# A list scheduler with new durations, a shared-port clock, more homes for filler weights, and a bias sum moved from ScalarE to VectorE

## The chip, the cores and the metric

The kernel runs on one core of a Trainium2 chip. The core has a matrix engine (TensorE, PE in the profile, with its weight loads as PEld), VectorE (DVE), ScalarE (ACT), GpSimd (POOL) and SyncE (SP), from whose queue every DMA of this kernel is issued. They share one memory of 128 partitions (SBUF); PE writes its results to eight accumulation banks (PSUM). The metric is the device time of one execution in microseconds.

## The reference, cut to what matters

One layer of a hybrid backbone over 1024 tokens of width 1024, with 256 context tokens. A modulated RMS norm is followed by one input projection; from it come a Fourier branch and a gated DeltaNet in two directions; both are merged by gates, and a ConvFFN of width 2816 follows. The part that the change touches is the DeltaNet's decay matrix:

```python
gc = jnp.cumsum(chunks(g), axis=-1)
decay = jnp.exp(jnp.where(lower_incl, gc[..., :, None] - gc[..., None, :], -jnp.inf))
kk = jnp.einsum('nbhcd,nbhsd->nbhcs', kc, kc)
l_mat = jnp.where(lower_strict, bc[..., :, None] * kk * decay, 0.0)
sol = lax.linalg.triangular_solve(l_mat, rhs, left_side=True, lower=True, unit_diagonal=True)
```

The kernel forms the decay as exp(-|g_j - g_i|) on a full 128 by 128 block and uses the triangle that it needs.

## The kernel before, in words

**A program that is recorded, ordered and then emitted.** `layer` calls engine methods, but these only record an `Op` (L172) with its operands and a `cost` (L247). `gates` adds what buffers impose: a tile in a region waits for the last reader of the tile that lay there before. `schedule` (L351) then walks a clock of its own: each engine has a time at which it is free, an operation is ready when its predecessors end plus a latency, and among those ready the one with the longest chain behind it (`rank`) goes next. The outcome is a fixed order on each engine, and the chip runs each engine's instructions strictly in that order, with waits between engines. So a number in `cost` moves no instruction's duration on the chip; it moves places in the order. All instructions carry the line of the one emitting call, L349 (L360 in the changed file), which is why the profile's groups are told apart by engine, tile kind and shape.

**The stages of the first half.** Ten stages in `ORDER` (two of context, c0 and c1, eight heads, x0 to x7) each go through: `project_kv` or `kq_head` (projections of 128 by 512 pieces, each value split in a high and a low part, hence three matmuls for a product), `decay_products`, `invert_blocks` (31 short VectorE steps), `merge_blocks` (chains of 32x32 and 64x64 matmuls named pa, pb, pc, pdd, pee) and a scan (`step`, L995: matmuls X and Y with VectorE and ScalarE between them). These chains leave PE without work, so a later stage's projections and the *fillers* of `side` (L1137: products z, g1, g0 and f that only the second half needs) are put between them.

**Fillers.** The weights of one filler are two halves of 128 by 512. Each half is loaded, copied rounded on ScalarE (the high part, tag `fh`) and subtracted on VectorE (the low part, in place of the load, tag `fl`). `WB` (L30) gives the number of homes: two for `fh`, three for `fl`. Results of all fillers go through one PSUM bank; the second group of 512 columns starts when ScalarE has evacuated the first.

**The decay (L796).** For each of two directions, a tile F of 128 by 8 by 128 is loaded with the row of cumulated logs broadcast over the partitions. Eight ScalarE instructions take |F + bias|, one for each 128 columns because the bias is another column vector each time; one more takes exp(-F). VectorE then multiplies F into the products kk, which start the inversion.

**The second half.** From about 1000 us on: output projections, then the FFN by a scheme of seven products with sums of weights on GpSimd (`both`, L1585), a 3 by 3 convolution on VectorE (`conv`, L1635), and the down projection.

Of the kernel before, what the change touches and what calls it, by code (L numbers as in the profile page):

```python
# [10 lines left out]
F32R = mybir.dt.float32r  # L11
AF = mybir.ActivationFunctionType
ALU = mybir.AluOpType
# [3 lines left out]
P = 128  # L17
# [9 lines left out]
AHEAD = 50  # L27
HALF = 512
WORDS = 53200
WB = {"H": 8, "L": 8, "h": 3, "l": 3, "fh": 2, "fl": 3, "woh": 8, "wol": 8, "dh": 3, "dl": 3, "LT": 2, "tk": 2}  # L30
DB = {"kn": 1, "vn": 1, "fs": 1}
ORDER = ("c0", "x0", "x1", "c1", "x2", "x3", "x4", "x5", "x6", "x7")
SIDES = (4, 4, 2, 2, 2, 2, 2, 2, 2, 2)
# [136 lines left out]


class Op:  # L172
    __slots__ = ("eng", "method", "args", "kw", "cost", "preds", "succs", "n", "ready", "rank", "start", "at", "ins", "bonus")

    def __init__(self, eng=None, method=None, args=(), kw=None, n=-1, cost=0.0):
        self.eng, self.method, self.args, self.kw, self.n, self.cost = eng, method, args, kw, n, cost
        self.preds, self.succs, self.ready, self.start, self.bonus = {}, [], 0.0, None, 0.0


def _meet(a, b):  # L180
# [8 lines left out]
class Program:  # L189
# [57 lines left out]
    def cost(self, eng, method, args, kw):  # L247
        out = args[0] if args else kw["out"]
        shape = out.shape
        n = math.prod(shape[1:])  # L250
        ins = [x for x in list(args[1:]) + list(kw.values()) if isinstance(x, View)]
        psum = any(v.slot.space == PSUM for v in ins)
        if eng == "PE":
            if method == "transpose":
                return max(53, args[1].shape[0] * 2 / 2.4 + 2)
            rhs, m = args[2], math.prod(args[1].shape[1:])
            n = max(math.prod(rhs.shape[1:]), m)
            if rhs.shape[0] <= 64 and m <= 64:
                return 34 if n <= 32 else 80
            return n / 2.4 + 3 if rhs.dtype == F32R and n >= 256 else n * 4 / 2.4 + 5  # L260
        if eng == "DVE":
            if method == "reciprocal":
                return 65 + 6.3 * n
            ptr = any(v.shape[-1] == 1 and v.arr.size <= P for v in ins) and method in ("tensor_scalar", "scalar_tensor_tensor")
            fast = method in ("tensor_copy", "tensor_scalar") and not psum and out.slot.space != PSUM
            return 66 + n / (1.92 if fast else 0.96) + (61 if ptr else 0)
        if eng == "ACT":
            aps = any(isinstance(kw.get(x), View) for x in ("scale", "bias", "accum_out"))
            return (51 if psum else 93) + n * 0.833 + (93 if aps else 0)
        if eng == "POOL":  # L270
            if method == "memset":
                return 36 + 0.83 * n
            if kw.get("op") == ALU.pow:
                return 300 + 165 * n
            if method == "tensor_copy":
                return 119 + 3.33 * n
            if method == "affine_select":
                return 1060
            return 140 + 2.12 * n
        run = 1  # L280
        view = out if isinstance(out, View) else args[1]
        if isinstance(view, View):
            a_ = view.arr
            for d in range(a_.ndim - 1, -1, -1):
                if a_.shape[d] > 1 and a_.strides[d] != run:
                    break
                run *= a_.shape[d]
        total = math.prod(shape) * 4
        return max(60.0, total / 359.0 * (1 if run * 4 >= 512 else 2))

    def record(self, engine, method, args, kw):
        op = Op(engine.name, method, args, kw, len(self.ops), self.cost(engine.name, method, args, kw))
        op.bonus = self.bonus
        out = args[0] if args else kw["out"]
        for k_, v in list(enumerate(args[1:])) + list(kw.items()):
            if isinstance(v, View) and k_ not in ("out", "accum_out"):
                self.access(op, v, False)
        for v in (out, kw.get("accum_out")):
            if isinstance(v, View):
                self.access(op, v, True)  # L300
        self.ops.append(op)
# [49 lines left out]
    def schedule(self):  # L351
# [7 lines left out]
        while todo:  # L359
            o = todo.pop()  # L360
# [11 lines left out]
            done += o.cost if o.eng == "PE" else 0.0  # L372
        left = {o: len(o.preds) for o in nodes}
        free = {n: 0.0 for n in self.eng}
        cold = 0.0
        wait, can = {n: [] for n in self.eng}, {n: [] for n in self.eng}
        count, dma, hw = 0, 0.0, 0.0
        issued = []
# [19 lines left out]
        for _ in range(len(ops)):  # L398
            best = None
            for n in self.eng:  # L400
                if can[n]:
                    t = free[n]
                elif wait[n]:
                    t = max(free[n], wait[n][0][0])
                else:
                    continue
                if best is None or t < best[0]:
                    best = (t, n)
            t, n = best
            while wait[n] and wait[n][0][0] <= t + AHEAD:  # L410
                _, c, o = heapq.heappop(wait[n])
                heapq.heappush(can[n], (-o.rank, c, o))
            o = heapq.heappop(can[n])[2]
            t = max(t, o.ready)
            o.start = t
            issued.append(o)
            if n == "SP":
                hw = max(hw, t + 50) + 460
                dma = max(dma, hw + 700) + o.cost
                free[n] = max(t + 60, dma - LEAD)  # L420
                end = dma
            else:
                cost = o.cost
                if n == "PE":
                    if t - free[n] > 3000:
                        cold = t + 4500
                    if t < cold:
                        cost *= 2
                free[n] = end = t + cost
            work = []  # L430
            for q in o.succs:
                settle(q, end + self.lat(o, q), work)
            release(work)
# [54 lines left out]
def layer(prog, a, out):  # L488
    te, ve, se, po, sp = (prog.eng[n] for n in ("PE", "DVE", "ACT", "POOL", "SP"))
# [4 lines left out]
    psum = pool("psum", bufs=2, space=PSUM)  # L494
# [143 lines left out]
    for q in range(4):  # L638
        n = (2, 4)[q // 2]
# [149 lines left out]
    NU = 8  # L789
# [6 lines left out]
    def decay_products(name, kT, co, cols, growsrc, qT=None):  # L796
        rk, b2, bk, c1 = co
        gcol = cols(ngc)
        Fs, LTs = [], []
        for d in range(2):  # L800
            F_ = dt("F", f"F_{name}{d}", (P, NU, P))
            src = growsrc(d)
            Ff = F_.rearrange("p u j -> p (u j)")
            sp.dma_start(Ff.rearrange("p (a b) -> p a b", a=src.shape[1]) if len(src.shape) == 3 else Ff, src)
            for u in range(NU):
                se.activation(F_[:, u, :], F_[:, u, :], AF.Abs, bias=gcol[:, d, u:u + 1])
            se.activation(F_, F_, AF.Exp, scale=-1.0)
            Fs.append(F_)
            LTs.append(dt("LT", f"L_{name}{d}", (P, NU, P)))
        for g in range(2):  # L810
            pt = ps("pd", [P, 4, P], f"kk_{name}{g}")
            for i in range(4):
                u = g * 4 + i
# [984 lines left out]
```

## Time and profile before

| | |
|---|---|
| median of three runs | 2051.59 us (2049.98 to 2053.32) |
| the profiled execution | 2047.95 us, its span 2046.2 us |
| PE busy | 1953.0 us, 95% |
| VectorE, ScalarE, GpSimd busy | 67%, 42%, 28% |
| mean granted PE clock | 0.979 |

PE is busy almost throughout. What is to be read is therefore where PE is not busy, what ended each such wait, and where its clock was granted at half. The profile's `m`, `p` and `d` stand for SBUF, PSUM and DRAM tiles; idle time in brackets is that just ahead of an instruction, with what ended it.

### The profile page before, as it was taken

What the parts mean: (1) busy time and instruction counts of PE and PEld (TensorE: products, weight loads), DVE (VectorE), ACT (ScalarE), POOL (GpSimd) and SP (SyncE); (2) the same over time, 40 slices, a digit from 0 to 9 for tenths busy, and PEclk for the clock granted to TensorE, in tenths of its full rate; (3) what the DMA queues carried; (4) which work ended last, traced back from release to release, by engine and by line L of the source; (5) the groups of instructions that cost most, each with busy time, mean ns of one, the idle gap of its engine ahead of it and who ended that gap; (6) DMA issues with size and microseconds to landing.
All of it is one profiled execution on the core that took longest, in us unless ns stands there. A gap on an engine that the chain in (4) does not pass through costs nothing.

```text
span 2046.2 us, 31495 instructions
## 1 busy us (share of the span) xinstructions
PE 1953.0 (95%) x11470; PEld 1570.9 (77%) x11470; DVE 1363.1 (67%) x2848; ACT 858.1 (42%) x2088; POOL 564.0 (28%) x573
## 2 busy tenths in 40 slices
PE   8989999899999999999999999979999999999998
PEld 3868888787777788778776778857878888878886
DVE  5648767667677577673655485479988889882132
ACT  5575354555354453632431032454444444532121
POOL 3110121101112220210221000257878888600000
PEclk9989999899999999999999999999999999999999
DMA  7153324344451543441778562312222222453231
GB/s 298 52 187 92 105 88 132 117 145 128 113 149 52 149 150 92 118 114 51 223 234 289 181 221 102 114 52 78 95 75 80 83 83 86 167 181 100 77 126 52
DMA packets 180637, 257.52 MB, mean 126 GB/s; under 512 B 75921, under 2 KB 97522, under 8 KB 180482
## 3 DMA queue, kind: packets, MB, share of 16 engines
q1 hardware_dynamic: 180482, 255.51, 39.0%
q8 instruction: 90, 1.47, 0.3%
q14 instruction: 65, 0.53, 0.1%
HBM read 194.52 MB, written 60.94 MB: 125 GB/s over the span
## 4 chain that ended last, share of the span: by engine, by line
PE 71%; DVE 14%; DMA 5%; ACT 5%; issue 2%; POOL 1%; SPq 0%; DVEq 0%; POOLq 0%; ACTq 0%
PE p L349 71%; DVE m L349 11%; ACT m L349 4%; DMA m<-d 3%; DVE p L349 3%; DMA d<-m 2%; ACT p L349 1%; POOL m L349 1%; DMA m<-in_w_ada_dram 1%; SPq L349 0%; DMA m<-in_wu_dram 0%; ACT L349 0%; DVEq L1787 0%; POOLq L1787 0%; DVEq L349 0%
## 5 line engine op out<-in xcount | busy, mean ns | idle before, releaser
L349 PE MATMUL p<-m,m 128*128 128x512 f32 (+7 forms) x11310 | 1937.8, 338 | 75.7 <-ACT m L349 31.6
L349 PEld LDWEIGHTS p<-m,m 128*128 128x128 f32 (+4 forms) x11310 | 1551.2, 174 | 452.6 <-ACT m L349 62.4
L349 DVE TENSOR_TENSOR m<-m,m 128x512 fp32r<-128x512 f32 (+27 forms) x1096 | 557.4, 523 | 253.4 <-ACT m L349 222.8
L349 ACT ACTIVATE m<-m 128x512 fp32r<-128x512 f32 (+8 forms) x649 | 411.3, 652 | 613.5 <-DMA m<-d 161.0
L349 POOL TENSOR_TENSOR m<-m,m 128x512 fp32r<-128x512 f32 (+5 forms) x338 | 449.5, 1353 | 782.6 <-DVE m L349 625.1
L349 ACT ACTIVATE m<-p 128x512 f32<-128x512 f32 (+5 forms) x510 | 221.1, 448 | 329.3 <-PE p L349 286.0
L349 DVE SCALAR_TENSOR_TENSOR m<-p,m,m 128x128 f32<-128x128 f32 (+4 forms) x488 | 203.1, 452 | 92.3 <-ACT m L349 40.9
L349 DVE SCALAR_TENSOR_TENSOR p<-m,m,p 128x512 f32<-128x512 f32 x352 | 240.1, 749 | 2.7 <-ACT p L349 0.4
L349 ACT ACTIVATE m<-p,m 128x128 f32<-128x128 f32 (+2 forms) x240 | 115.7, 495 | 184.3 <-PE p L349 179.5
L349 POOL MEMSET m<- 128x1024 f32 (+7 forms) x79 | 35.7, 460 | 381.7 <-PE p L349 224.0
L349 POOL COPY m<-m 32x256 f32<-32x256 f32 (+2 forms) x136 | 60.3, 447 | 211.5 <-DMA m<-d 173.7
L349 DVE SCALAR_TENSOR_TENSOR m<-m,m 128x512 f32<-128x512 f32 (+5 forms) x119 | 65.7, 558 | 28.6 <-ACT m L349 16.3
L349 DVE COPY m<-p 32x256 f32<-32x256 f32 (+11 forms) x116 | 42.1, 368 | 62.5 <-PE p L349 32.8
L349 DVE TENSOR_TENSOR m<-p,m 128x512 f32<-128x512 f32 (+4 forms) x91 | 57.8, 645 | 30.5 <-PE p L349 29.1
L349 DVE SCALAR_TENSOR_TENSOR m<-m,m,m 128x1024 f32<-128x1024 f32 (+2 forms) x68 | 59.6, 878 | 26.0 <-DMA m<-in_w_ada_dram 25.6
L349 DVE TENSOR_TENSOR m<-m,p 128x128 f32<-128x128 f32 (+3 forms) x117 | 53.4, 458 | 29.6 <-PE p L349 28.8
L349 ACT ACTIVATE p<-p 128x128 f32<-128x128 f32 x208 | 55.4, 266 | 25.6 <-PE p L349 23.6
L349 DVE SCALAR_TENSOR_TENSOR m<-m,p 128x512 f32<-128x512 f32 x76 | 50.7, 682 | 13.9 <-ACT m L349 7.7
L349 DVE SCALAR_TENSOR_TENSOR m<-m,m,p 128x128 f32<-128x128 f32 x128 | 42.7, 342 | 23.5 <-PE p L349 22.8
L349 ACT ACTIVATE m<-m,m 128x128 f32<-128x128 f32 (+1 forms) x168 | 54.6, 406 | 6.3 <-DMA m<-d 3.6
L349 POOL TENSOR_SCALAR_AFFINE_SELECT m<-m 128x1024 f32<-128x1024 f32 x16 | 18.9, 1199 | 100.4 <-DVE m L349 100.4
L349 DVE SCALAR_TENSOR_TENSOR m<-m 128x1 f32<-128x1 f32 (+1 forms) x25 | 4.7, 188 | 54.3 <-ACT m L349 54.2
(20 smaller groups left out, 210.3 us busy)
## 6 DMA issues: line engine op xcount, KB each, us to landing
m<-d SPq DMA_DIRECT2D x76, 512.0 KB
d<-m SPq DMA_DIRECT2D x138, 256.0 KB
m<-d SPq DMA_DIRECT2D x114, 256.0 KB
m<-in_wi_dram SPq DMA_DIRECT2D x106, 256.0 KB
m<-in_w_ada_dram SPq DMA_DIRECT2D x48, 512.0 KB
m<-in_wu_dram SPq DMA_DIRECT2D x88, 256.0 KB
m<-in_wn_dram SPq DMA_DIRECT2D x26, 512.0 KB
m<-d SPq DMA_DIRECT2D x44, 192.0 KB
```

Of the source, the lines that this page charges most:

```text
L349: return getattr(engine.real, method)(*[real(v) for v in args], **{k_: real(v) for k_, v in kw.items()})
```

## The change

Four edits:

1. The table `cost`: PE's 512-wide rounded product goes from n/2.4 + 3 to 0.4375 n + 4.5 ns (216 to 228.5 ns in the table), other products and transposes likewise; short strided VectorE sums get their own row; a ScalarE instruction with an accumulator gets 32 ns more.
2. `schedule` has one more clock, `port`: an operation marked in `record` (GpSimd work other than fills and powers, and VectorE work on SBUF alone that reads two tiles, copies or scales) is booked not before the last marked one ends.
3. `WB`: three homes for `fh`, four for `fl`.
4. In `decay_products` one VectorE sum over the whole 128 by 1024 tile adds the bias, and one ScalarE instruction takes the absolute value.

```diff
-WB = {"H": 8, "L": 8, "h": 3, "l": 3, "fh": 2, "fl": 3, "woh": 8, "wol": 8, "dh": 3, "dl": 3, "LT": 2, "tk": 2}
+WB = {"H": 8, "L": 8, "h": 3, "l": 3, "fh": 3, "fl": 4, "woh": 8, "wol": 8, "dh": 3, "dl": 3, "LT": 2, "tk": 2}
@@ cost
-                return max(53, args[1].shape[0] * 2 / 2.4 + 2)
+                return max(55, args[1].shape[0] * 0.86)
-            return n / 2.4 + 3 if rhs.dtype == F32R and n >= 256 else n * 4 / 2.4 + 5
+            return n * 0.4375 + 4.5 if rhs.dtype == F32R and n >= 256 else n * 1.75 + 4
+            if method == "tensor_tensor" and n < 200 and any(v.arr.ndim == 3 and v.arr.strides[-1] != 1 and v.shape[-1] > 1
+                                                             for v in ins):
+                return 60 + 1.75 * n
-            return (51 if psum else 93) + n * 0.833 + (93 if aps else 0)
+            return (51 if psum else 93) + n * 0.833 + (93 if aps else 0) + (32 if "accum_out" in kw else 0)
@@ record
+        if engine.name == "POOL":
+            op.port = method != "memset" and kw.get("op") is not ALU.pow
+        elif engine.name == "DVE" and all(v.slot.space is None for v in reads):
+            big = sum(math.prod(v.shape[1:]) > 1 for v in reads)
+            op.port = math.prod(out.shape[1:]) > 32 and (big > 1 or method in ("tensor_copy", "tensor_scalar"))
@@ schedule
-            t = max(t, o.ready)
+            t = max(t, o.ready, port if o.port else 0.0)
+            if o.port:
+                port = t + o.cost
@@ decay_products
-            for u in range(NU):
-                se.activation(F_[:, u, :], F_[:, u, :], AF.Abs, bias=gcol[:, d, u:u + 1])
+            ve.tensor_tensor(F_, F_, gcol[:, d, :].rearrange("p (u o) -> p u o", o=1).broadcast_to([P, NU, P]), op=ALU.add)
+            se.activation(F_, F_, AF.Abs)
             se.activation(F_, F_, AF.Exp, scale=-1.0)
```

The order moves on every engine in the first half, and little in the second. Three places follow.

**Place 1: ScalarE ahead of the evacuation of filler z0's first group.** Before: m_191 and m_197 are head 2's two F tiles, p_173 a square for the output norm, m_518<-p_124 a query projection's evacuation, m_4380<-p_126 the filler's.

```order
L349 ACTIVATE m_191<-m_191,m_1051 128x128 x7
L349 ACTIVATE m_197<-m_197,m_1051 128x128 x8
L349 ACTIVATE m_191<-m_191 128x1024
L349 ACTIVATE m_197<-m_197 128x1024
L349 ACTIVATE p_173,m_1115<-p_173 128x128
L349 ACTIVATE m_518<-p_124,m_328 128x512
L349 ACTIVATE m_4380<-p_126 128x512
```

Now (m_188 and m_195 are the F tiles, p_97 a square of the query norm, m_4303<-p_126 the filler's evacuation):

```order
L360 ACTIVATE m_188<-m_188 128x1024
L360 ACTIVATE p_97,m_839<-p_97 128x128
L360 ACTIVATE m_188<-m_188 128x1024
L360 ACTIVATE p_97,m_839<-p_97 128x128
L360 ACTIVATE m_195<-m_195 128x1024
L360 ACTIVATE p_97,m_839<-p_97 128x128
L360 ACTIVATE m_195<-m_195 128x1024
L360 ACTIVATE p_97,m_839<-p_97 128x128
L360 ACTIVATE m_539<-p_122,m_312 128x512
L360 ACTIVATE m_4303<-p_126 128x512
```

Sixteen instructions of 128 columns have become two of 1024; the two exponents still stand ahead of the evacuation.

**Place 2: PE at the first stage's kk, and VectorE behind it.** On PE before, p_97<-m_284 is kk, p_124 the first group of a value projection, p_126 its second:

```order
L349 MATMUL p_124<-m_200,m_479 128x512
L349 MATMUL p_124<-m_115,m_507 128x512
L349 MATMUL p_97<-m_284 128x128 x4
L349 MATMUL p_126<-m_401,m_497 128x512
L349 MATMUL p_126<-m_120,m_497 128x512
```

Now the 24 products of the second group (the last two are shown) and four of a query projection stand ahead of kk:

```order
L360 MATMUL p_126<-m_198,m_475 128x512
L360 MATMUL p_126<-m_115,m_513 128x512
L360 MATMUL p_122<-m_399,m_487 128x512
L360 MATMUL p_122<-m_119,m_487 128x512
L360 MATMUL p_122<-m_399,m_582 128x512
L360 MATMUL p_122<-m_129,m_487 128x512
L360 MATMUL p_97<-m_273 128x128 x4
```

kk reads a tile that is loaded from DRAM after the key tile of the fourth head (m_723 now) has been stored. On VectorE now, two of the new sums (m_195 and m_221, 128x1024) stand among the last operations on that key tile, which followed each other before:

```order
L360 SCALAR_TENSOR_TENSOR m_723<-p_122,m_312,m_723 128x511
L360 TENSOR_TENSOR m_195<-m_195,m_1056 128x1024
L360 SCALAR_TENSOR_TENSOR m_723<-m_794,m_312,m_723 128x1
L360 SCALAR_TENSOR_TENSOR m_723<-m_238,m_723 128x512
L360 TENSOR_TENSOR m_221<-m_221,m_1035 128x1024
L360 SCALAR_TENSOR_TENSOR m_723<-m_231,m_723 128x512
L360 SCALAR_TENSOR_TENSOR m_723<-m_238,m_723 128x256
```

kk has moved 28 products back, and its data depends on two more VectorE instructions.

**Place 3: PE in head 0's merge.** Before, between the products pa (p_103 from m_423 and m_773) and pb (p_103 from m_737) stand four products of a key projection (p_124), and fifteen in the whole merge:

```order
L349 MATMUL p_103<-m_423,m_110 32x32
L349 MATMUL p_103<-m_773,m_139 32x32
L349 MATMUL p_124<-m_162,m_490 128x512
L349 MATMUL p_124<-m_101,m_542 128x512
L349 MATMUL p_124<-m_205,m_490 128x512
L349 MATMUL p_124<-m_107,m_490 128x512
L349 MATMUL p_103<-m_737,m_773 32x32
```

Now only two products of the context scan stand there, and no 512-wide product in the whole merge:

```order
L360 MATMUL p_103<-m_428,m_110 32x32
L360 MATMUL p_103<-m_771,m_136 32x32
L360 MATMUL p_172<-m_342,m_141 128x128
L360 MATMUL p_174<-m_344,m_141 128x128
L360 MATMUL p_103<-m_736,m_771 32x32
```

In the other merges the count of 512-wide products goes from 27 to 31 (c0), 0 to 0 (x1), 28 to 32 (c1), 28 to 30 (x2), 20 to 28 (x3), 28 to 26 (x4), 27 to 27 (x5), 25 to 25 (x6) and 25 to 31 (x7).

More of the change, by code (lines that the diff above doesn't have):

```diff
@@ L172 @@
 class Op:
-    __slots__ = ("eng", "method", "args", "kw", "cost", "preds", "succs", "n", "ready", "rank", "start", "at", "ins", "bonus")
+    __slots__ = ("eng", "method", "args", "kw", "cost", "preds", "succs", "n", "ready", "rank", "start", "at", "ins", "bonus", "port")
     def __init__(self, eng=None, method=None, args=(), kw=None, n=-1, cost=0.0):
@@ L177, in __init__ @@
         self.preds, self.succs, self.ready, self.start, self.bonus = {}, [], 0.0, None, 0.0
+        self.port = False
 def _meet(a, b):
@@ L294, in record @@
         out = args[0] if args else kw["out"]
+        reads = [v for k_, v in list(enumerate(args[1:])) + list(kw.items())
+                 if isinstance(v, View) and k_ not in ("out", "accum_out")]
+        if engine.name == "POOL":
[3 more added lines that the diff above has]
+            op.port = math.prod(out.shape[1:]) > 32 and (big > 1 or method in ("tensor_copy", "tensor_scalar"))
         for k_, v in list(enumerate(args[1:])) + list(kw.items()):
@@ L374, in schedule @@
         free = {n: 0.0 for n in self.eng}
-        cold = 0.0
+        cold = port = 0.0
         wait, can = {n: [] for n in self.eng}, {n: [] for n in self.eng}
```

## The prediction, made before the changed kernel ran

> **What bounds the kernel now.** First the busy time by stage (columns: stretch, its length, then for PE, PEld, VectorE, ScalarE and GpSimd the busy time and the count of instructions, then granted clock, DMA share, GB/s).
>
> ```profile
> 100.00:1000.00 900.00, 851.23 (x6699) 705.77 (x6697) 614.90 (x1752) 443.54 (x1357) 144.48 (x240) 0.97 0.40 119
> 1300.00:1500.00 200.00, 179.39 (x755) 141.19 (x754) 165.60 (x225) 91.12 (x171) 131.20 (x101) 0.97 0.25 86
> 1500.00:1770.00 270.00, 270.00 (x1192) 223.45 (x1191) 240.41 (x334) 115.00 (x195) 221.89 (x168) 1.00 0.24 81
> ```
>
> From 1500 to 1770 us PE is never idle: 270.00 / 1192 = 0.2265 us for a 512-wide product, the price of one more or less in the path. No reorder of VectorE or GpSimd buys anything there. In the DeltaNet's 900 us PE is idle for 48.8 us, and at the FFN's start (1300 to 1500) for 20.6 us. Who ended PE's waits in the 900 us:
>
> ```profile
> PE p L349 <- ACT m L349: 15.5, 11, 4.2
> PE p L349 <- DMA m<-d: 14.3, 7, 8.7
> PE p L349 <- DVE m L349: 14.2, 22, 2.3
> ```
>
> Then the clock. These are the stretches of the 900 us in which it was granted at half:
>
> ```profile
> 142.70:156.40 13.70, 8.63 (x27) 7.07 (x28) 6.78 (x24) 13.69 (x39) 2.45 (x3) 0.50 0.47 154
> 388.50:405.50 17.00, 10.30 (x111) 8.15 (x112) 8.92 (x15) 11.72 (x27) 2.88 (x5) 0.50 0.31 105
> 477.20:484.00 6.80, 5.67 (x14) 4.31 (x15) 4.04 (x7) 3.24 (x6) 1.64 (x1) 0.50 0.62 116
> 610.30:624.00 13.70, 7.93 (x139) 5.45 (x140) 6.88 (x11) 4.37 (x9) 6.46 (x12) 0.50 0.29 75
> 682.00:685.40 3.40, 3.40 (x9) 2.68 (x9) 1.75 (x3) 2.15 (x4) 1.90 (x2) 0.50 0.72 154
> 825.40:828.80 3.40, 3.40 (x70) 2.24 (x70) 3.40 (x5) 1.04 (x3) 3.18 (x5) 0.50 0.99 283
> ```
>
> Half of PE's busy time inside them is lost: 39.33 / 2 = 19.7 us. So 48.8 + 19.7 = 68.5 us is all that a better order could win in the 900 us. Five of the six largest waits of PE there, one row each of the timeline:
>
> ```profile
> 147.25 2.08 PE L349 MATMUL p<-m 128*128 128x128 f32 x8 [8.74 <-DMA m<-d]
> 478.33 1.22 PE L349 MATMUL p<-m,m 128*128 128x512 f32 x2 [3.47 <-ACT m L349]
> 612.38 1.22 PE L349 MATMUL p<-m,m 128*128 128x512 f32 x2 [4.18 <-ACT m L349]
> 681.74 1.85 PE L349 MATMUL p<-m,m 128*128 128x512 f32 x4 [2.47 <-ACT m L349]
> 825.34 2.10 PE L349 MATMUL p<-m,m 32*32 32x32 f32 x6 [2.06 <-DMA m<-d]
> ```
>
> Each is followed or overlapped by one of the half-clock stretches. Ahead of three of them ScalarE does the same thing; here is the one at 478 us, then the one at 682 us:
>
> ```profile
> 470.54 4.50 ACT L349 ACTIVATE m<-m,m 128x128 f32<-128x128 f32 x15
> 474.94 2.00 ACT L349 ACTIVATE m<-m 128x1024 f32<-128x1024 f32 x2
> ...
> 477.68 0.59 ACT L349 ACTIVATE m<-p 128x512 f32<-128x512 f32 x1
> ```
>
> ```profile
> 674.24 4.79 ACT L349 ACTIVATE m<-m,m 128x128 f32<-128x128 f32 x16
> 678.92 2.01 ACT L349 ACTIVATE m<-m 128x1024 f32<-128x1024 f32 x2
> ...
> 681.10 0.59 ACT L349 ACTIVATE m<-p 128x512 f32<-128x512 f32 x1
> ```
>
> The sixteen biased absolute values and two exponents run ahead of a filler's evacuation (the last row), and PE's next group of that filler waits for its one bank. So part of PE's idle time is a ScalarE queue, not a lack of work.
>
> **Term 1, the sixteen absolute values (edit 4).** What takes their place is in these rows:
>
> ```profile
> L349 ACT ACTIVATE m<-m,m 128x128 f32<-128x128 f32 x160 | 50.5, 397 | 3.6 <-DMA m<-d 3.6
> L349 ACT ACTIVATE m<-m 128x1024 f32<-128x1024 f32 x46 | 47.1, 1056 | 10.2 <-DMA m<-d 5.0 <-DMA m<-in_x_dram 3.2 <-DMA m<-in_ctx_dram 1.8
> L349 DVE TENSOR_TENSOR m<-m,m 128x1024 f32<-128x1024 f32 x36 | 44.5, 1248 | 13.0 <-ACT m L349 12.6
> ```
>
> ScalarE's block goes from 4.79 us to 2 x 1.056 = 2.11 us, 2.7 us shorter. Applied to the three waits, and at most the wait itself: 2.7 + 2.7 + 2.47 = 7.9 us. The half clock behind them costs (5.67 + 7.93 + 3.40) / 2 = 8.5 us; I take 6 of it, since the 1.5 us left at 612 us and the merge right behind it may still hold the clock down. Together 13.9 us. Below: nothing, if the new order puts another evacuation behind the exponents. Above: 10.1 + 8.5 = 18.6 us.
>
> The Trainium skill, "TensorE: Matmul & The Clock Gate", section "What's actually happening", says that the clock falls back only after at least one idle window of about 3.4 us. By it the waits that remain would cost no clock and the term would be 7.9 + 8.5 = 16.4 us. The trace agrees on the length of the stretches (3.40, 6.80, 13.70) but not on the cause: a wait of 2.06 us stands just ahead of the stretch at 825.4.
>
> **Term 2, kk behind 28 products (edit 1).** At the order's second place, 28 x 0.2265 = 6.3 us of the 8.74 us wait would be filled. Two sums of 1.25 us now stand ahead of the store that the load waits for, so 6.3 - 2.5 = 3.8 us. The stretch from 142.7 costs 8.63 / 2 = 4.3 us of clock; a wait of some 5 us remains, so I take half, 2.1. Together 5.9 us. Below: nothing, if the second group's bank is still waiting for ScalarE. Above: 8.7 + 4.3 = 13 us.
>
> **Term 3, the homes (edit 3).** With two homes a filler's first high half can be made only when the filler before it has used its own first half. The waits that end with such a copy alone:
>
> ```profile
> 532.65 1.65 PE L349 MATMUL p<-m,m 128*128 128x512 f32 x6 [0.69 <-ACT m L349]
> 906.77 1.55 PE L349 MATMUL p<-m,m 128*128 128x512 f32 x6 [0.44 <-issue]
> 1072.42 1.91 PE L349 MATMUL p<-m,m 128*128 128x512 f32 x7 [1.11 <-ACT m L349]
> ```
>
> 0.69 + 0.44 + 1.11 = 2.2 us. Below nothing, above 2.2 plus what of the 4.18 us at 612 us term 1 leaves, 3.7 us.
>
> **Term 4, head 0's merge loses its cover (edit 1).** Fifteen products leave it: 15 x 0.2265 = 3.4 us that PE now waits in a chain of small products, and a half-clock stretch of 3.4 us would add 1.7. Cost 5.1 us. The merge at 388.5 to 405.5 had no such product before, and is the longest half-clock stretch; if head 0's became like it, (17.0 - 10.3) + 10.3 / 2 = 11.9 us, the upper bound. Below: nothing, if the context scan's own products fill it.
>
> **Term 5, 20 sums on VectorE.** 20 x 1.25 = 25 us, in a stretch where it is idle for 900 - 614.9 = 285 us. That slack is the cover: PE waits for VectorE for only 14.2 us there. Without it all 25 us would be in the path, which is the upper bound; zero is the lower. A sum does not wait long for its F tile: ScalarE waited 3.6 us in all for them. I take 2 us, nearer the row of 14.2 us of waits over 614.9 us of work (2.3%, or 0.6 us), and more than it because a sum of 1.25 us blocks a chain of 0.35 us steps for longer.
>
> **What I cost at nothing.** The clock for the port (edit 2) changes the order of GpSimd hardly at all, and in the FFN the cover is PE itself, busy for 270.00 of 270.00 us; with that gone, the 20.6 us before 1500 show what is at stake either way. That VectorE and GpSimd do hold each other off is in these rows of 1500 to 1770 us, the same operation with two SBUF operands and with one in PSUM:
>
> ```profile
> L349 DVE TENSOR_TENSOR m<-m,m 128x512 f32<-128x512 f32 x28 | 39.1, 1429 | 0.1
> L349 DVE TENSOR_TENSOR m<-m,p 128x512 f32<-128x512 f32 x28 | 19.2, 684 | 0.8 <-PE p L349 0.4
> ```
>
> The edit does not stop this, it only books it. The new sums read two SBUF tiles too, but in the DeltaNet GpSimd is busy for 144.48 of 900 us, 16%.
>
> **The sum.** -13.9 - 5.9 - 2.2 + 5.1 + 2.0 = -14.9 us. The profiled execution took 2047.95 us around its span of 2046.2; the median is 3.6 us above it. Taken off the median: 2051.6 - 14.9 = 2036.7 us.
>
> **The rivals.**
>
> *The queue on ScalarE was most of it.* The order is then better everywhere: all of PE's waits for ScalarE and for DMA in the 900 us (15.5 + 14.3) and the half clock (19.7) go, 49.5 us at most, and with two thirds of it 2018.6 us. For it: three of the six largest waits are one pattern. Against: head 1's merge has no filler before or after, and the DMA waits are round trips through DRAM.
>
> *The waits only move.* Every stage's order is new, and a gap closed at one place opens at another: the gains of terms 1 to 3 (22.0 us) against an equal number of new gaps, 2051.6 us. For it: head 0's merge, which lost what the first kk got. This is also the case in which the change does not do what it says, because ScalarE's evacuations come late for another reason.
>
> *The sums sit in the chain.* VectorE runs in order; a sum whose F tile is late holds every scan step behind it. With all 25 us in the path, merges as in term 4's upper bound (11.9) and term 1 and 2 at half (9.9): 25 + 11.9 - 9.9 = +27 us, 2078.6 us; with 15 us of the sums in the path it is +17, 2068.6 us, which I give as its time. It decides from 15 us on, that is 0.75 us for each sum (then 15 + 5.1 - 19.8 = 0.3). For it: at kk two sums stand on the very chain that PE waits for. Against: 285 us of slack.
>
> *The sums and GpSimd lock each other out.* Both then stretch: a sum of 1.25 us can hold each of the merge's GpSimd copies. Twenty sums met at each, 25 us more on top of the forecast, 2061.7 us; GpSimd's 16% makes it 4 us. The Trainium skill, "SBUF — State Buffer", section "SBUF: two separate sides", has this as a rule: whichever of the two starts first holds the shared pair for its whole instruction, and the other is blocked. The 1429 against 684 ns above agree.
>
> **How the numbers follow.** A kernel of this spread (2049.98 to 2053.32) can't be told from no change within about 0.2%, 4.1 us. Forecast 0.45; the larger gain 0.20; waits that only move 0.16; the sums in the chain 0.15; the lock 0.04. Of the forecast's cases 0.42 lie beyond -4.1 us and 0.03 within; of the moving waits 0.04 are faster, 0.08 the same, 0.04 slower; the sums in the chain are slower, the lock half the same. Faster 0.42 + 0.20 + 0.04 = 0.66; same 0.03 + 0.08 + 0.02 = 0.13; slower 0.04 + 0.15 + 0.02 = 0.21. The forecast's own range goes from the upper ends of terms 1 to 3 (11.8 + 1.5 = 13.3 us more) to half of terms 1 and 2 (9.9 us less): 2023.4 to 2046.6. The range for all holds the larger gain down to 2012 and the slower cases up to 2062, which leaves out about 0.2.
>
> **What would show it.** Right: ScalarE's blocks of sixteen gone, and no wait of PE over 2 us behind the two exponents; PE idle in the first 900 us under 40 us; fewer than six half-clock stretches there; the FFN from 1500 us on the same within 1 us. Wrong: PE's waits ended by VectorE well above 14.2 us with a 128x1024 sum ahead of them (the sums in the chain); idle time and stretches as many as before at other places (waits that move); or a wait at head 0's merge of over 5 us, which would make term 4 the largest.

## The result, and the profile after

The changed kernel takes 2041.55 us (median of 5 runs, 2033.99 to 2043.51) against 2053.32 us (2049.98 to 2057.14) of the kernel before, run beside it: ratio 0.9936, 95% interval 0.9918 to 0.9955, or 11.8 us faster by the medians. (Differences in us between other runs, below, are their ratios to the kernel before, taken times 2050 us.) The profiled execution took 2041.67 us, its span 2040.0 us; that of before was 2047.95 and 2046.2 us, a short one among its runs, so the two traces explain 6.2 us of span and not the whole 11.8.

Busy time by stage in the changed kernel, columns as in the prediction:

```profile
100.00:1000.00 900.00, 858.15 (x6717) 706.12 (x6717) 635.01 (x1778) 414.97 (x1214) 135.74 (x241) 0.98 0.40 120
1500.00:1770.00 270.00, 270.00 (x1186) 221.75 (x1186) 242.44 (x334) 118.00 (x199) 221.08 (x171) 1.00 0.25 84
```

PE's idle time in the 900 us goes from 48.8 to 41.9 us. In the FFN from 1500 to 1770 us PE is never idle, as before. Now the span up to 1000 us, divided behind head 1's merge, before and after:

```profile
0.00:420.00 420.00, 385.26 (x2638) 306.61 (x2639) 274.98 (x713) 228.80 (x619) 72.14 (x108) 0.96 0.42 135
420.00:1000.00 580.00, 555.68 (x4489) 457.98 (x4487) 397.52 (x1165) 269.97 (x828) 95.53 (x159) 0.98 0.40 118
```

```profile
0.00:420.00 420.00, 380.76 (x2618) 304.24 (x2619) 280.76 (x716) 217.02 (x562) 69.30 (x108) 0.95 0.41 133
420.00:1000.00 580.00, 566.12 (x4532) 460.97 (x4531) 412.72 (x1190) 254.29 (x747) 87.49 (x160) 1.00 0.41 121
```

The first 420 us got worse (idle 34.7 to 39.2 us), the rest better (24.3 to 13.9 us). The half-clock stretches say the same. Those of the changed kernel between 100 and 1000 us are these four, 40.9 us long, where before there were six of 58.0 us:

```profile
141.30:144.70 3.40, 3.40 (x10) 2.62 (x9) 1.47 (x4) 3.20 (x17) 0.00 (x0) 0.50 0.75 222
291.50:301.70 10.20, 6.62 (x19) 5.30 (x20) 5.23 (x11) 2.92 (x11) 1.96 (x1) 0.50 0.07 27
387.10:411.00 23.90, 13.50 (x203) 10.69 (x190) 12.41 (x18) 10.32 (x16) 7.84 (x14) 0.50 0.36 130
434.90:438.30 3.40, 3.40 (x16) 3.07 (x15) 1.99 (x6) 1.97 (x7) 0.00 (x0) 0.50 0.39 146
```

Those at 477, 610, 682 and 825 us are gone: after 420 us half of PE's busy time in such stretches is 1.7 us, from (5.67 + 7.93 + 3.40 + 3.40) / 2 = 10.2. The two at the merges of heads 0 and 1 are new or longer: between 100 and 420 us it is (3.40 + 6.62 + 13.50) / 2 = 11.8 us, from (8.63 + 10.30) / 2 = 9.5. Who ended PE's waits in the 900 us:

```profile
PE p L360 <- DVE m L360: 16.0, 23, 4.8
PE p L360 <- ACT m L360: 9.5, 16, 1.5
PE p L360 <- DMA m<-d: 7.5, 8, 2.2
PE p L360 <- ACT p L360: 6.1, 4, 2.7
```

Where the three waits of term 1 (3.47, 4.18 and 2.47 us) were, PE now waits 1.45, 0.89 and 0.34 us:

```profile
483.12 1.16 PE L360 MATMUL p<-m 128*128 128x128 f32 x8 [1.45 <-ACT p L360]
```

```profile
620.45 1.88 PE L360 MATMUL p<-m,m 128*128 128x512 f32 x7 [0.89 <-ACT m L360]
```

```profile
692.67 1.65 PE L360 MATMUL p<-m,m 128*128 128x512 f32 x6 [0.34 <-ACT m L360]
```

The first of these is no longer the filler's. It is a later kk, which waits for ScalarE's squares in its bank (`ACT p`); the filler's products follow at 484.17 us without a wait. Ahead of the third, ScalarE now runs seven rounded copies of weights (6.46 us) and no exponents.

The first kk's wait of 8.74 us is gone, and the second group's products wait 2.15 us in its place. With the 28 products ahead of it kk starts at 148.07 us, where it was 147.25 before:

```profile
140.00 8.23 PE L360 MATMUL p<-m,m 128*128 128x512 f32 x28 [2.15 <-DVE m L360]
148.07 1.05 PE L360 MATMUL p<-m 128*128 128x128 f32 x8
```

Head 0's merge and what follows it had two waits of PE before, 1.2 us together:

```profile
290.32 2.05 PE L349 MATMUL p<-m,m 128*128 128x128 f32 x14 [0.22 <-DVE m L349]
293.37 6.84 PE L349 MATMUL p<-m,m 128*128 128x128 f32 x32 [1.00 <-DVE m L349]
```

and has four now, 6.1 us together:

```profile
287.12 1.15 PE L360 MATMUL p<-m,m 64*64 64x64 f32 x32 [0.41 <-DVE m L360]
289.01 1.15 PE L360 MATMUL p<-m,m 64*64 64x64 f32 x32 [0.75 <-ACT m L360]
292.38 2.08 PE L360 MATMUL p<-m,m 128*128 128x128 f32 x8 [2.23 <-DMA m<-d]
297.16 3.33 PE L360 MATMUL p<-m,m 128*128 128x512 f32 x7 [2.70 <-ACT p L360]
```

At head 1's merge the longest wait of the 900 us is one behind the new sums. First VectorE there, then PE:

```profile
390.15 1.23 DVE L360 TENSOR_TENSOR m<-m,m 128x1024 f32<-128x1024 f32 x1 [3.41 <-DMA m<-d]
391.41 0.42 DVE L360 COPY m<-p 32x256 f32<-32x256 f32 x1
391.86 1.30 DVE L360 TENSOR_TENSOR m<-m,m 128x1024 f32<-128x1024 f32 x1
393.19 0.43 DVE L360 COPY m<-p 32x256 f32<-32x256 f32 x1
```

```profile
393.68 1.06 PE L360 MATMUL p<-m,m 32*32 32x32 f32 x32 [4.76 <-DVE m L360]
396.31 0.79 PE L360 MATMUL p<-m,m 128*128 128x128 f32 x2 [1.57 <-DMA m<-d]
```

The two 1024-wide rows are sums. The first sum's F tile was late (VectorE idle for 3.41 us, ended by a DMA), the merge's two copies stand behind the sums, and PE waits for the copies.

### The profile page after: what moved, and what is told of

It reads as the page before. It is cut to its first block, busy times and chain, and to the rows that moved or that the text cites. A ratio compares the mean times of both kernels' runs of the same rounds, so it can differ in the third digit from the quotient of the medians.

```text
span 2040.0 us, 31321 instructions
## 1 busy us (share of the span) xinstructions
PE 1955.1 (96%) x11470; PEld 1568.0 (77%) x11470; DVE 1383.6 (68%) x2868; ACT 829.6 (41%) x1948; POOL 548.3 (27%) x573
## 4 chain that ended last, share of the span: by engine, by line
PE 73%; DVE 11%; DMA 8%; ACT 4%; issue 2%; POOL 1%; SPq 1%; DVEq 0%; POOLq 0%; ACTq 0%
PE p L360 73%; DVE m L360 10%; DMA m<-d 4%; ACT m L360 4%; DMA d<-m 2%; DMA m<-in_w_ada_dram 1%; DVE p L360 1%; POOL m L360 1%; SPq L360 1%; DMA m<-in_wd_dram 0%; ACT p L360 0%; DMA m<-in_wi_dram 0%; ACT L360 0%; DVEq L1800 0%; POOLq L1800 0%
## 5 line engine op out<-in xcount | busy, mean ns | idle before, releaser
L360 PE MATMUL p<-m,m 128*128 128x512 f32 (+5 forms) x11310 | 1940.6, 338 | 75.3 <-DVE m L360 33.9
L360 PEld LDWEIGHTS p<-m,m 128*128 128x128 f32 (+3 forms) x11310 | 1549.7, 173 | 457.5 <-ACT m L360 60.0
L360 DVE TENSOR_TENSOR m<-m,m 128x512 fp32r<-128x512 f32 (+27 forms) x1116 | 579.8, 536 | 238.0 <-ACT m L360 209.0
L360 ACT ACTIVATE m<-m 128x512 fp32r<-128x512 f32 (+8 forms) x669 | 430.5, 662 | 631.5 <-DMA m<-d 165.5
L360 POOL TENSOR_TENSOR m<-m,m 128x512 fp32r<-128x512 f32 (+5 forms) x338 | 441.9, 1334 | 899.3 <-DVE m L360 729.3
L360 ACT ACTIVATE m<-p 128x512 f32<-128x512 f32 (+4 forms) x510 | 218.8, 447 | 315.1 <-PE p L360 287.0
L360 POOL COPY m<-m 32x256 f32<-32x256 f32 (+2 forms) x136 | 53.8, 399 | 200.8 <-DMA m<-d 172.2
L360 DVE SCALAR_TENSOR_TENSOR m<-m,m,p 128x128 f32<-128x128 f32 x128 | 42.7, 340 | 25.4 <-PE p L360 24.8
L360 ACT ACTIVATE p<-m,m 128x512 f32<-128x512 f32 x44 | 30.2, 691 | 39.4 <-DVE m L360 39.3
L360 ACT ACTIVATION_READ_ACCUMULATOR p<-p 128x1 f32 x208 | 39.3, 189 | 0.0
```

The source lines that it names most:

```text
L360: return getattr(engine.real, method)(*[real(v) for v in args], **{k_: real(v) for k_, v in kw.items()})
```

## The experiments

The prediction read a gain off the shorter ScalarE block, and the trace fits it. But each edit also makes the planner write a new order on every engine, so the first four runs change an operation and keep the order, the next five change edits and let the planner order anew, and the last three change the order and nothing else. All ratios are to the kernel before, run beside them. The diffs of the first four runs are abridged to the lines that change what runs; `swap` makes those who waited for one operation wait for another.

### The shorter block alone, in the order before

The eight biased absolute values of a tile are one without bias, at the last one's place (the bias is left out of the decay, to price the block alone):

```diff
         issued = self.schedule()
+        for name, (F_, bias) in self.bias.items():
+            eight = [o for o in issued if o.eng == "ACT" and o.args[0].slot.name == name and o.args[2] is AF.Abs]
+            one = Op("ACT", "activation", (F_, F_, AF.Abs), {})
+            issued[issued.index(eight[-1])] = one
+            self.swap(issued, set(eight), [one])    # who waited for the eight waits for the one
+            issued = [o for o in issued if o not in eight]
```

> The order of the kernel before on every engine, unchanged; only the eight biased absolute values of each F tile are one instruction of 1024 columns without bias, at the place of the last of the eight (no sum anywhere: the bias is left out of the decay). It prices the shorter ScalarE block alone. Theory A, the ScalarE queue (term 1): the three waits at 478, 612 and 682 us shrink or go, with the half clock behind them, -13.9 us, 2039 us against 2053 (at least 8 us faster). Theory B, the new order is the gain: the waits shrink by what term 1 says at most in part, and PE waits elsewhere instead, under 4 us faster.

Measured: 2048.17 us, ratio 0.9991 (0.9978 to 1.0005): 1.8 us faster (between 4.5 faster and 1.0 slower), where term 1 had said 13.9. The same three places of PE, from 472, 604 and 676 us on:

```profile
474.86 0.96 PE L349 MATMUL p<-m,m 128*128 128x512 f32 x3 [0.97 <-ACT m L349]
477.45 2.94 PE L349 MATMUL p<-m,m 128*8 128x128 f32 x7 [1.63 <-POOL m L349]
```

```profile
609.36 0.72 PE L349 MATMUL p<-m,m 128*128 128x512 f32 x2 [2.70 <-ACT m L349]
612.22 0.31 PE L349 MATMUL p<-m,m 32*32 32x32 f32 x2 [2.14 <-DMA m<-d]
```

```profile
681.12 2.09 PE L349 MATMUL p<-m,m 32*32 32x32 f32 x65 [2.44 <-DMA m<-d]
```

The kernel before had this row behind its wait of 4.18 us:

```profile
614.52 0.31 PE L349 MATMUL p<-m,m 32*32 32x32 f32 x2 [0.92 <-DMA m<-d]
```

And the waits of its 900 us:

```profile
PE p L349 <- DMA m<-d: 17.3, 6, 8.7
PE p L349 <- DVE m L349: 15.5, 24, 2.1
PE p L349 <- ACT m L349: 8.8, 9, 2.7
PE p L349 <- issue: 2.5, 1, 2.5
```

The mechanism is there: waits for ScalarE fall from 15.5 to 8.8 us. The gain isn't: what PE does next then waits for something else. At 612 us the wait for the evacuation is 1.48 us shorter, and the one behind it, for the merge's load of the inverted blocks, 1.22 us longer. Waits for DMA, VectorE and the issue rise by 3.0, 1.3 and 2.1 us, and 1.6 us for GpSimd are new.

Since PE's order is the same in both kernels, each of its instructions can be timed against itself. In the two traces this run is ahead of the kernel before by 0.8 us at 470 and 1.2 at 486 us, by 1.5 at 600 and 2.3 at 618, by 2.9 at 660 and 4.0 at 690: the three places are worth 2.4 us in all. At 883 us it is 4.8 us ahead, and from 1106 us on not at all. The lead goes at two later waits, each with a half-clock stretch (904.0 to 907.5 and 1102.0 to 1105.4 us) that the kernel before doesn't have there. A wait of 0.44 us ahead of a filler (at 906.77 us before) is now

```profile
904.47 7.74 PE L349 MATMUL p<-m,m 128*128 128x512 f32 x85 [2.51 <-issue]
```

and one of 1.68 us for ScalarE (at 1102.01 us before) is 2.66 us. So theory B holds here and theory A falls: in a fixed order the second latest releaser is close behind ScalarE, and most of what still comes through is lost further on.

### Edit 4 whole, in the order before

The same kernel with the sum on VectorE, in the place where its first absolute value stood in time:

```diff
+            s = Op("DVE", "tensor_tensor", (F_, F_, bias), {"op": ALU.add})
+            s.preds, one.preds = one.preds, {s: True}
+            issued.insert(issued.index(eight[0]), s)
```

> The order before, unchanged, with edit 4 alone: the sum stands on VectorE at the time at which the first of the eight absolute values stood on ScalarE, and one absolute value of 1024 columns takes the place of the last of them. Against the run without the sum it prices the 20 sums in an order that was not made for them. Theory A (term 5): 2 us more than without the sum. Theory C, the sums sit in the chain: 5 us more or above, with a wait of PE for VectorE behind a 128x1024 sum.

Measured: 2057.93 us, ratio 1.0045 (1.0028 to 1.0062). Against the run without the sums that is 0.0054, 11 us, and 9 us slower than before: term 5's 2 us was far off for sums that the order hasn't made room for.

### The changed kernel without the sums, its order kept

```diff
         issued = self.schedule()
+        for s in [o for o in issued if o.eng == "DVE" and o.method == "tensor_tensor"
+                  and o.args[0].slot.name.startswith("F_") and o.kw["op"] == ALU.add]:
+            self.swap(issued, {s}, list(s.preds))   # who waited for the sum waits for its load
+            issued.remove(s)
```

> The order of the changed kernel on every engine, unchanged, with the 20 sums left out (the decay lacks its bias). It prices term 5 as it stands. Theory A: 2 us faster than the changed kernel's 2041.5 us. Theory C: the wait of 4.76 us at head 1's merge (388.9 us), where the inputs of a product are copied by VectorE behind a sum whose F tile was late, goes, and part of the half-clock stretch of 23.9 us there: 5 to 10 us faster.

Measured: 2041.50 us, ratio 0.9957 (0.9943 to 0.9971), no faster than the changed kernel's 0.9936 (0.9918 to 0.9955). Head 1's merge on PE there:

```profile
391.23 1.06 PE L360 MATMUL p<-m,m 32*32 32x32 f32 x32 [2.36 <-DVE m L360]
396.13 1.10 PE L360 MATMUL p<-m,m 128*128 128x128 f32 x4 [3.84 <-DMA m<-d]
```

The wait of 4.76 us shrinks to 2.36, and the next, for the scan's state from DRAM, grows from 1.57 to 3.84 us; its products start at 396.13 in place of 396.31 us. So theory C falls: where the planner made room for them, 20 sums cost nothing that these runs can tell (the two intervals overlap), and the most visible wait behind one of them covers a load that ends the stretch anyway.

### The old block in the changed order

```diff
         issued = self.schedule()
+            for u in range(8):
+                o = Op("ACT", "activation", (F_[:, u, :], F_[:, u, :], AF.Abs), {"bias": gcol[u]})
+                eight.append(o)
+            i = issued.index(one)                   # the absolute value of 1024 columns
+            issued[i:i + 1] = eight
+            issued.remove(s)                        # the sum
```

> The order of the changed kernel, unchanged, with edit 4 undone in place: no sums, and eight biased absolute values of 128 columns where the one of 1024 columns stood on ScalarE. Theory A: ScalarE's block is 2.7 us longer again ahead of the evacuations, 8 to 14 us slower than the changed kernel, less the 2 us of the sums, so 2048 to 2054 us. Theory B: the new order does not mind, within 4 us of 2041.5 us. Theory C: faster than the changed kernel, 2037 us or below.

Measured: 2061.57 us, ratio 1.0063 (1.0043 to 1.0082): 0.0127 or 26 us slower than the changed kernel, nearly twice what theory A said. PE's waits in its 900 us:

```profile
PE p L360 <- ACT m L360: 16.6, 20, 3.1
PE p L360 <- DVE m L360: 16.5, 23, 3.9
PE p L360 <- ACT p L360: 10.7, 5, 3.1
```

Waits for ScalarE rise from 9.5 + 6.1 to 16.6 + 10.7 us. So the length of the block decides at most 4.5 us in the order before and 26 us in the order after. An order is fitted to the operations that it was made for. The loss comes stage by stage: in the traces, 19.9 us apart in span, the same instruction of PE is late by 3.7 us at 170, 7.2 at 490, 9.7 at 622, 14.9 at 696 and 19.0 at 836 us. Ten stages of 2.7 us would be 27 us, so a block that grows in a fitted order is paid for in most of them.

### Edits in other sets, each with an order of its own

Each is the kernel before with only some hunks of the change. Edit 4 alone, against before:

```diff
-            for u in range(NU):
-                se.activation(F_[:, u, :], F_[:, u, :], AF.Abs, bias=gcol[:, d, u:u + 1])
+            ve.tensor_tensor(F_, F_, gcol[:, d, :].rearrange("p (u o) -> p u o", o=1).broadcast_to([P, NU, P]), op=ALU.add)
+            se.activation(F_, F_, AF.Abs)
```

> The kernel before with edit 4 alone, and the order made anew for it. The order then already has the first kk behind the second group of the value projection and no 512-wide product in head 0's merge, which the prediction had put down to edit 1. The first four runs showed that in a given order the shorter block is worth 2 us and that an order made for other operations loses 9 to 13 us. Theory F (the order belongs to its operations, and edit 4 is what made the gain, through the order): 8 to 13 us faster than before, near the changed kernel. Theory G (edits 1 to 3 made the gain): within 4 us of before.

Measured: 2031.33 us, ratio 0.9909 (0.9895 to 0.9924), 18.7 us faster than before and faster than the whole change. The 900 us:

```profile
100.00:1000.00 900.00, 863.51 (x6753) 712.14 (x6752) 640.58 (x1783) 420.20 (x1224) 141.98 (x242) 0.98 0.40 121
```

PE is idle for 36.5 us, from 48.8. In this kernel kk has already moved (22 products back) and head 0's merge has lost its 512-wide products, which the prediction had put down to edit 1.

Edits 1 to 3, against the changed kernel:

```diff
-            ve.tensor_tensor(F_, F_, gcol[:, d, :].rearrange("p (u o) -> p u o", o=1).broadcast_to([P, NU, P]), op=ALU.add)
-            se.activation(F_, F_, AF.Abs)
+            for u in range(NU):
+                se.activation(F_[:, u, :], F_[:, u, :], AF.Abs, bias=gcol[:, d, u:u + 1])
```

> The changed kernel without edit 4 (eight biased absolute values on ScalarE), with the order made anew: kk is back ahead of the second group and twelve 512-wide products are in head 0's merge. Theory F: 2048 to 2055 us, within 4 us of before. Theory G: 8 us or more faster than before.

Measured: 2051.48 us, ratio 1.0008 (0.9996 to 1.0021). That is what theory F said, and theory G falls.

Edit 1 alone, against before (one row of the table stands for the hunk):

```diff
-            return n / 2.4 + 3 if rhs.dtype == F32R and n >= 256 else n * 4 / 2.4 + 5
+            return n * 0.4375 + 4.5 if rhs.dtype == F32R and n >= 256 else n * 1.75 + 4
```

> The kernel before with the new table of costs alone, and the order made anew: kk ahead of the second group, seventeen 512-wide products in head 0's merge. Theory F: within 4 us of before (2047 to 2055). Theory G, with truer durations: 8 us or more faster. Theory H (every new order is a draw, some 5 us to either side, whatever the edit): anything from 2042 to 2060, and the four runs of this set don't add up to the whole.

Measured: 2040.39 us, ratio 0.9955 (0.9942 to 0.9968), 9.2 us faster. That contradicts the last run if edits add up: edits 2 and 3 would have to cost 11 us between them.

The change without edit 3, against the changed kernel:

```diff
-WB = {"H": 8, "L": 8, "h": 3, "l": 3, "fh": 3, "fl": 4, ...
+WB = {"H": 8, "L": 8, "h": 3, "l": 3, "fh": 2, "fl": 3, ...
```

> The changed kernel with two and three homes for the filler weights again, and the order made anew; up to 430 us it is the changed kernel's own. Term 3 says 2.2 us slower than the changed kernel (0 to 3.7), from the waits with which fillers start. Theory H: up to 5 us to either side.

Measured: 2047.11 us, ratio 0.9990 (0.9979 to 1.0000), 11 us slower than with edit 3, three times the upper bound of term 3.

The change without edit 2, against the changed kernel:

```diff
-            t = max(t, o.ready, port if o.port else 0.0)
+            t = max(t, o.ready)
```

> The changed kernel without edit 2 (no clock for the port), with the order made anew: some 2800 of PE's 9401 places differ. The prediction cost edit 2 at nothing: within 4 us of the changed kernel, ratio 0.992 to 0.996 to the kernel before. Theory I (edit 2 or 3 is what turns edit 4's 0.991 into 0.994): ratio 0.990 or below. Theory H (a new order is a draw): 0.988 to 0.999.

Measured: 2038.82 us, ratio 0.9937 (0.9917 to 0.9956), the changed kernel's own 0.9936. Edit 2 is worth nothing here, so theory I fails for it, with some 2800 of PE's 9401 places taken by a product of another tile. Either edit 2 or edit 3 must then have cost much in one set and nothing in another, unless a new order is itself worth some 10 us.

### A new order and nothing else

The planner treats an operation as ready that becomes so within 50 ns. That number means nothing on the chip:

```diff
-AHEAD = 50
+AHEAD = 45
```

In the changed kernel it is 55, in the one with edit 4 alone 45.

> The kernel before with one number of the planner that means nothing on the chip changed: it looks 45 ns ahead for ready operations in place of 50. 2013 of PE's 9401 places differ; durations, homes and operations are the same. It prices a new order for its own sake. Theory F (the operations make the gain): within 4 us of before. Theory H (a draw): 5 us or more to either side.

Measured: 2039.91 us, ratio 0.9949 (0.9932 to 0.9966): 10.5 us faster than before, with no edit.

> The same on the changed kernel, 55 ns in place of 50: 2143 of PE's places differ, the first kk and head 0's merge as in the changed kernel. Theory F: 2037 to 2046 us, ratio 0.992 to 0.996. Theory H: outside of that by 3 us or more.

Measured: 2049.60 us, ratio 0.9988 (0.9971 to 1.0005): 11 us slower than the changed kernel, its gain gone. One place shows a large part of how. ScalarE at the evacuation of filler z5's first group (the row of 128x512) in the changed kernel, whose PE waited 0.89 us there:

```profile
618.86 1.06 ACT L360 ACTIVATE m<-m 128x1024 f32<-128x1024 f32 x1
619.82 0.58 ACT L360 ACTIVATE m<-p 128x512 f32<-128x512 f32 x1
620.30 3.89 ACT L360 ACTIVATE m<-m 128x1024 f32<-128x1024 f32 x4
```

and in this run, ScalarE and then PE:

```profile
617.01 5.93 ACT L360 ACTIVATE m<-m 128x1024 f32<-128x1024 f32 x6 [0.74 <-DVE m L360]
622.85 0.57 ACT L360 ACTIVATE m<-p 128x512 f32<-128x512 f32 x1
```

```profile
623.48 3.93 PE L360 MATMUL p<-m,m 128*128 128x512 f32 x8 [6.34 <-ACT m L360]
```

The evacuation stands second in the row of 1024-wide operations in the one order and last in the other. That is 5.45 us, and a half-clock stretch of 6.8 us (620.5 to 627.3) begins inside the wait. The block is the short one in both. The draw of the kernel before has the same wait with the long block, 8.41 us where before had 4.18, and is 10.5 us faster all the same:

```profile
602.75 4.78 ACT L349 ACTIVATE m<-m,m 128x128 f32<-128x128 f32 x16 [0.17 <-DMA m<-d]
607.43 3.88 ACT L349 ACTIVATE m<-m 128x1024 f32<-128x1024 f32 x4
```

```profile
611.85 2.71 PE L349 MATMUL p<-m,m 128*128 128x512 f32 x6 [8.41 <-ACT m L349]
```

> The same on the kernel with edit 4 alone, 45 ns in place of 50: 1156 of PE's places differ. If edit 4's 18.7 us belong to the operations (theory F), the ratio stays at 0.988 to 0.994. Theory H: 0.994 to 0.999, a lucky draw before.

Measured: 2030.21 us, ratio 0.9903 (0.9887 to 0.9919), as good as its first order.

### What the twelve runs say together

The ten kernels whose order the planner made, by ratio:

| | old table | new table (edit 1) |
|---|---|---|
| without edit 4 | 1.0000 (before), 0.9949 (its draw) | 0.9955, 1.0008 |
| with edit 4 | 0.9909, 0.9903 (its draw) | 0.9936, 0.9988 (its draw), 0.9990, 0.9937 |

Six with edit 4 have a mean of 0.9944, four without 0.9978: 7 us, with a standard error of 4.4 us from their scatter. So theory H holds for the size of most differences, and that edit 4 gains at all is likely and not shown by this. Edit 4 with the old table is the lowest of all in both its orders. Whether the new table, edit 2 or edit 3 takes back what edit 4 gives stays open: those two orders differ from the four on the right by more than one edit, and two draws are few.

Where the lead arises can be read too. Count at each moment the work that PE has still to do (228 ns for a 512-wide product, 118 or 112 for each record of a 256- or 128-wide one, about what they take in these traces at full clock without a wait, and a rough 30 for a smaller one; that makes 1852.2 us in every kernel), and ask how much sooner a kernel's trace has the same amount left than the kernel before (in us, good to 1 or 2):

| lead over the kernel before | at 550 us | at 750 us | at 1000 us | at 2000 us |
|---|---|---|---|---|
| the changed kernel | -3.3 | 7.8 | 6.2 | 6.3 |
| its draw | -1.0 | 3.4 | -2.3 | -1.9 |
| edits 1 to 3 | 0.0 | 5.8 | -2.7 | -1.3 |
| edit 1 alone | 0.9 | 7.8 | -0.7 | 7.4 |
| edit 4 alone | 3.2 | 9.4 | 12.1 | 16.3 |
| draw of the kernel before | 5.2 | 8.6 | 9.9 | 8.8 |

The changed kernel makes its lead between 550 and 750 us, where the kernel before has the waits of 4.18 and 2.47 us. But every new order wins there, with the old long block too: 5.8, 6.9 and 3.4 us in the three kernels without edit 4. So a good part of the gain is that the kernel before had drawn an order that is bad at this place. Edit 1 alone loses that lead again and has its 7.4 us from elsewhere: 1.2 at 1300 us and 7.6 at 1600, from the FFN's start.

The version to take is edit 4 alone, 18.7 and 19.9 us faster than before in two orders.

## Why the prediction came out as it did

The sign and the size were right, 2041.55 for 2036.7 us, and the case forecast as likeliest is the one whose signs the trace shows. The explanation behind it was only half right, and the size was in part luck: the same change in another order took 2049.60 us, outside the forecast's 2023.4 to 2046.6.

**Term 1 (-13.9) is what the trace shows, and not for the reason given.** The waits fell by 10.12 - 2.68 = 7.4 us (7.9 was forecast) and the clock behind them came back. The step that failed is "2.7 us shorter, applied to the three waits". In the order before, that shortening alone was worth 1.8 us, and 2.4 us of PE's time at the three places, since GpSimd or a load comes close behind ScalarE there (waits of 1.63, 2.14 and 2.44 us). The step left out the next releaser. What closed the waits was another place of the evacuation in ScalarE's order, as z5 shows: 0.89 or 6.34 us with the same short block.

Nor did ScalarE do the same thing ahead of all three. At the longest wait, that of 4.18 us, it had itself waited for its F tiles' loads, and five more operations of 1024 columns (2.00 and 2.50 us) stood ahead of the evacuation:

```profile
602.18 2.46 ACT L349 ACTIVATE m<-m,m 128x128 f32<-128x128 f32 x8 [2.69 <-DMA m<-d]
604.94 2.46 ACT L349 ACTIVATE m<-m,m 128x128 f32<-128x128 f32 x8 [0.30 <-DMA m<-d]
```

**Terms 2 (-5.9) and 4 (+5.1) are undersized, and both are edit 4's.** The wait of 8.74 us became one of 2.15, and of the stretch's 4.3 us of clock 1.7 are left: 6.6 + 2.6 = 9.2 us, within its 13. Head 0's merge lost 0.22 + 1.00 us before (the waits at 290.32 and 293.37 us) and now 6.1, with 3.3 us of clock: 8.2 us, within its 11.9. Their net was forecast as -0.8 and came out as -1.0, as two errors that cancel. That both come with edit 4 the orders show: with edits 1 to 3 kk stands in its old place and twelve 512-wide products are in the merge. The prediction put them down to edit 1 from the order of the whole change, where the edits can't be told apart.

**Term 3 (-2.2)** can't be told from a draw: 11 us in the one comparison, beside 11 us for 5 ns of look-ahead.

**Term 5 (+2.0)** is 0 within the noise in the order made for it, and 11 us in one that wasn't. Head 1's merge got the wait that the rival of the sums in the chain foretold (4.76 us, from a late F tile), but a load from DRAM set the end of that stretch, as the run without the sums showed. The waits for VectorE went from 14.2 to 16.0 us only.

**What was costed at nothing.** Edit 2 was worth nothing in the end (0.9937 without it, 0.9936 with it), and the FFN gave nothing from 1600 us on: the lead is 6.5 us there and 6.3 at 2000.

**The rival that waits only move** had 0.16. For this order it was wrong, and as an account of the kernel it was the best: the same change with another look-ahead is 0.9988. Its price should have been a spread of some 10 us to either side of any forecast, since each edit draws a new order.

**What would show it.** The blocks of sixteen went; PE's longest wait for ScalarE's results in SBUF is 1.5 us; there are four half-clock stretches for six. No single wait at head 0's merge is over 5 us (the longest is 2.70), but the four make 6.1. PE's idle time of 41.9 us missed the 40 that was named, by what the two merges took back.

## What to carry to other kernels

Where a planner writes the order, an edit's effect is its own worth plus a draw. Before an edit is credited, change a number that means nothing, and see how far the time moves: here 10 us in two kernels of three, as much as the result, and 1.2 us in the third. To find an operation's own price keep the order fixed, and ask at each wait which releaser comes second: a wait shortens only down to that one, and a lead that is won can be lost at a later wait. And test the edits alone; the whole change was some 6 us worse than one part of it.

## What the runs showed of the hardware that was not expected

**The clock falls without a long wait.** In the changed kernel it is at half from 291.5 to 301.7 us, where PE is busy for 6.62 of 10.20 us and no wait is over 2.70 us, and for 23.9 us from 387.1, where PE is busy for 13.50 us in small products with waits between them; that stretch begins 1.8 us before its longest wait (4.76 us). A merge without cover costs twice: its waits, and half of what runs in them. The Trainium skill, "TensorE: Matmul & The Clock Gate", section "What's actually happening", gives one idle window of about 3.4 us as the condition; read as PE idle throughout, no such window is in the first of these stretches or just ahead of it.

What does stand ahead of all four stretches in the 900 us is a window in which PE is busy for less than half: 1.32, 1.31, 1.25 and 1.66 us in the 3.413 us before 141.3, 291.5, 387.1 and 434.9. The lengths of the stretches are multiples of 3.413 us. Divide the 14 traces of this case from 100 us on into windows of that length, in step with the clock's changes, and the busy share of a window at full clock tells what follows it:

| PE busy in the window | windows | followed by half clock |
|---|---|---|
| under 40% | 95 | 95 |
| 40 to 50% | 40 | 27 |
| 50 to 60% | 50 | 8 |
| 60 to 80% | 201 | 7 |
| over 80% | 7299 | 0 |

At half clock, none of 124 windows with PE busy for under 80% was followed by full clock, and 125 of 135 with more were. So here a wait costs clock when it makes a window less than about half busy, and short waits add up to that.

**PE's busy time isn't a constant of the work.** Of the changed kernel's 14.7 us gained in idle time and clock over the whole span (idle 93.3 to 84.9 us, half of the busy time at half clock 29.1 to 22.8 us), 8.4 us are given back inside PE's busy time: 1953.0 - 29.1 = 1923.9 us at full clock before, 1955.1 - 22.8 = 1932.3 after, for the same 11470 instructions. By the same account all eight kernels with the new table, those with a kept order too, lie at 1930.2 to 1934.2 us, and the six with the old one at 1920.7 to 1927.1. Short waits that hide under the modelled end of the product ahead count as work: a 128x128 product behind a visible wait is booked with 377 ns in the changed kernel (the median of 59 records), and one without a wait, behind another of its shape, with 112 ns. The hidden ones can be counted. Take the 128- and 512-wide records at full clock that have a semaphore to wait for, no visible idle time, and more than 30 ns over the usual 112 or 228 ns: there are 131 of them before and 210 after, and their excess goes from 19.3 to 25.4 us, 6.1 of the 8.4 us. The kernels with the old table have 131 to 150, those with the new one 193 to 216. So most of what was given back is waiting that no idle row shows. Why the new table makes more of it was not tested.
